# Eight split-weight buffers at eight starting offsets, and convolution taps halved in place

## The chip, the cores and the metric

The kernel runs on one core of a Trainium2 chip. The metric is the device time of one execution in microseconds. An execution of the program is also taken with the hardware profiler; its span reaches from the first to the last instruction, and the device time of that execution is a little longer.

## The reference

Four trunk layers work on 256 latent tokens and 256 context tokens of 1024 channels. Layers 0 and 3 mix tokens with a two-directional state-space scan, layer 1 with windowed attention, layer 2 with a chunked gate; each is followed by a gated feed-forward part. Everything is float32. Cut to what matters here:

```python
for i in range(DEPTH):                       # 4
    a = modulate(rms_norm(h, norm_g[i, 0]), sh1, sc1)
    h = h + g1 * mixer[i % 3](a)             # scan, attention, gate
    h = h + g2 * swiglu(modulate(rms_norm(h, norm_g[i, 1]), sh2, sc2), ffn_w_in[i], ffn_w_out[i])
return rms_norm(h_lat, final_g)

# inside the scan mixer, before the scan:
xbc = silu(depthwise_conv(zxbcdt[..., 2048:5120], conv_w, conv_b))   # 5 taps along the tokens
```

## The kernel before

**Products in three.** A float32 product is made of three products of a shorter format (F32R). A weight `w` is split into `hi`, which is `w` rounded to that format, and `lo = w - hi`; an activation is split in the same way. `mm3` (lines 163 to 167) issues, for each 128 x 128 block of weights, `hi` with the activation's high part (L165), `hi` with its low part (L166) and `lo` with its high part (L167). In the value parts of layers 1 and 2 (tile `vp`) the split weights are the moving operand and the activations the stationary one; everywhere else the weights are the stationary one, and 512 or 256 (258 in one stage) token columns stream past.

**The order of the weights.** `make_plan` lists all 454 weight chunks of the program in the order of use. `get(idx)` (L158) hands out one chunk's buffers and first calls `pump` (L143), which brings the chunks up to two ahead: a DMA into one of 3 `raw` buffers (L140), then, in pieces of 512 columns, a cast on ScalarE into `hi` (L152) and a subtraction into `lo` (L154) on VectorE, in the scan stages partly on GpSimd. There are 4 `hi` and 4 `lo` buffers of 1024 words, taken in turn, so a buffer is rewritten four chunks later, once the products that read it are done.

**Where the buffers lie.** All offsets are bytes within a partition. The three `raw` buffers start at 45056, 49152 and 53248, the four `hi` at 57344, 61440, 65536 and 69632, the four `lo` at 73728, 77824, 81920 and 86016, the split activations `a_hi` and `a_lo` at 90112 and 106496. All these are multiples of 2048, and so are the tiles of the stages behind them (`hh`, `hl`, `gh`, `gl`, `xw`, `bm` and others, from 122880 on). Tiles are laid end to end, rounded up to 32 bytes. The scan stage's small tiles end at 229312 of 229376.

**The taps.** The parameters lie in the tile `par`, brought by the first DMA (L115). Its columns from `C_CW` to `C_NW` hold the taps and biases of the convolution: 5 x 24 taps for each of the two scan layers, then 24 biases for each, 288 columns in all. `ssd_scan` makes a tile `hw` of 6 x 24 columns with six multiplications by 0.5 (L746 to L749), once in layer 0 and once in layer 3. `conv` (L751) reads its taps and bias from `hw`, one column as a scalar for each instruction: a ScalarE activation (L757), four VectorE instructions (L761), and then `y (1 + tanh y)`, for which the half is wanted.

**Order of instructions.** The kernel is written as a data flow; a scheduler puts each engine's instructions in order by priority and estimated time and may pull an instruction with no unmet need far ahead of its place in the text. Each engine then works through its queue in order.

Of the kernel before, what the change touches and what calls it, by code (L numbers as in the profile page):

```python
# [8 lines left out]
F32 = mybir.dt.float32  # L9
F32R = mybir.dt.float32r  # L10
# [3 lines left out]
ALU = mybir.AluOpType  # L14
# [3 lines left out]
P = 128  # L18
# [47 lines left out]
SC_MM = (3,)  # L66
SC_FROM = 4
SPLIT_BUFS = 4
TAIL_POOL = (5, 7)


# [3 lines left out]
C_CW = C_FG + 8  # L75
C_CB = C_CW + 2 * 5 * 24
C_NW = C_CB + 2 * 24
# [22 lines left out]
class Builder:  # L100
    def __init__(self, ctx, tc, ap):
        self.ctx, self.tc, self.nc, self.ap = ctx, tc, tc.nc, ap
        nc = self.nc
        pool = lambda name, bufs=1, **kw: ctx.enter_context(tc.tile_pool(name=name, bufs=bufs, **kw))
        self.cp = pool("cp")
        self.sp = pool("sp", 2)
        self.wp = pool("wp")
        self.dp = pool("dp", space=bass.MemoryType.DRAM)
        self.pm = pool("pm", 3, space=PSUM)
        self.ps = pool("ps", 3, space=PSUM)  # L110
        self.pt = pool("pt", 2, space=PSUM)
        cp = self.cp

        self.par = cp.tile([P, NPAR + PAD], F32, name="par")[:, :NPAR]
        nc.sync.dma_start(self.par, ap["pars"])  # L115
        self.k0 = cp.tile([P, NK0], F32, name="k0")
        nc.sync.dma_start(self.k0, ap["consts"][:, 0:NK0])
        self.h = [cp.tile([P, KD, HT], F32, name=f"h{i}") for i in range(2)]
        for i in range(2):
            nc.sync.dma_start(self.h[i], ap["xin"][i])  # L120
        self.ident = self.k0[:, K_ID : K_ID + P]
        self.ones = self.k0[:, K_ONE : K_ONE + P]
        self.a_hi = self.a_lo = None
        self.acc, self.sqlast = {}, None

        self.plan = []
        self.ready = {}
        self.emitted = 0
        self.ahead = 2
        self.lo_eng = nc.vector  # L130
        self.lo_alt = None
# [11 lines left out]
    def pump(self, upto):  # L143
        nc = self.nc
        while self.emitted < min(upto + 1, len(self.plan)):
            src, n = self.plan[self.emitted]
            raw = self.load(src, n)
            hi = self.wp.tile([P, 1024], F32R, tag="hi", name="hi", bufs=SPLIT_BUFS)
            lo = self.wp.tile([P, 1024], F32R, tag="lo", name="lo", bufs=SPLIT_BUFS)
            for p0 in range(0, n, PIECE):  # L150
                sl = slice(p0, min(n, p0 + PIECE))
                nc.scalar.copy(hi[:, sl], raw[:, sl])  # L152
                eng = self.lo_eng if self.lo_alt is None or p0 == 0 else self.lo_alt
                eng.tensor_tensor(out=lo[:, sl], in0=raw[:, sl], in1=hi[:, sl].bitcast(F32), op=ALU.subtract)  # L154
            self.ready[self.emitted] = (hi, lo)
            self.emitted += 1
# [540 lines left out]
    def ssd_scan(self, layer, jj, lat_only, sp, first, turn_out):  # L697
        nc = self.nc
        par = self.par
# [42 lines left out]

        turn = []


        hw = self.ss.tile([P, 6, 24], F32, name="hw")  # L746
        for k in range(6):
            c = C_CW + (jj * 5 + k) * 24 if k < 5 else C_CB + jj * 24
            nc.vector.tensor_scalar(hw[:, k, :], par[:, c : c + 24], 0.5, None, ALU.mult)  # L749

        def conv(t, a, b, o, dst):  # L751
            w = lambda k: hw[:, k, t : t + 1]
            y = dst
            nh = (b - a) // HT
            yv = y[:, a:b].rearrange("p (h t) -> p h t", h=nh)
            ov = o.rearrange("p (h t) -> p h t", h=nh)
            nc.scalar.activation(y[:, a:b], o, AF.Identity, bias=w(5), scale=w(2))  # L757
            for k in (0, 1, 3, 4):
                s = k - 2
                d0, d1 = max(0, -s), HT - max(0, s)  # L760
                nc.vector.scalar_tensor_tensor(  # L761
                    yv[:, :, d0:d1], ov[:, :, d0 + s : d1 + s], w(k), yv[:, :, d0:d1], ALU.mult, ALU.add
                )
            th = sp.tile([P, T], F32, tag="xt", name="th", bufs=SS_BUFS["xt"])[:, a:b]
            nc.scalar.activation(th, y[:, a:b], AF.Tanh)
            nc.vector.scalar_tensor_tensor(y[:, a:b], th, 1.0, y[:, a:b], ALU.add, ALU.mult)

        def epi_x(m, a, b, o):
            xt = sp.tile([P, T], F32, tag="xt", name="xt", bufs=SS_BUFS["xt"])
            conv(m, a, b, o, xt)  # L770
            flush()
            turn.append((m, a, b, xt))
# [14 lines left out]
        def bc(i):  # L787

            def epi(m, a, b, o):
                flush()  # L790
                tag = ("bt", "ct")[i % 2]
                dst = (bt, ct)[i % 2][i // 2] = sp.tile([P, T], F32, tag=tag, name=tag, bufs=SS_BUFS[tag])
                conv(16 + 4 * (i % 2) + i // 2, a, b, o, dst)
                mod_step()

            self.linear([ids["bc"][i]], range(KD), self.rhs_a, epi, toks=tlat if i % 2 else ((0, T),))
# [57 lines left out]
        for d in range(2):  # L854
            w = self.ss.tile([P, 4, 32], F32, name=f"wdt{d}")
# [549 lines left out]
    def build(self):  # L1405
# [69 lines left out]
        for m in range(KD):  # L1475
            fg = self.par[:, C_FG + m : C_FG + m + 1]
            if m in TAIL_POOL:
                nc.gpsimd.tensor_scalar(o[:, m, :], self.h[LAT][:, m, :], fg, None, ALU.mult)
# [126 lines left out]
```

## Time and profile before

| | |
|---|---|
| median of 3 runs | 2669.74 us (2665.63 to 2680.74) |
| the profiled execution | 2673.48 us |
| its span | 2671.7 us |
| TensorE products / weight loads, count | 13672 / 13672 |
| mean granted TensorE clock | 0.990 |
| DMA moved | 353.57 MB, 132 GB/s in the mean |

In the profile, PE is TensorE's products and PEld its weight loads, DVE is VectorE, ACT ScalarE, POOL GpSimd, SP the queue that issues the DMAs. A line number such as L165 is a line of the kernel before. In a group's row, `out<-in` names the tiles, `x` the count, and the two numbers behind the bar are the busy time in us and the mean of one in ns. A row of the timeline has the start, the time in us, the engine, the line and the operation, and in brackets the idle time of the engine before it and what ended it. The time of one product in a row overlaps with that of the next, since products are pipelined; how fast they follow each other is read from their starts. A row of one tile's instructions has the shortest, the median and the longest time in ns. A row of busy time by windows has, for each engine, busy us and the number of instructions.

### The profile page before, as it was taken

To read this page: it belongs to the slowest core of one execution; us is meant where nothing else is said; L and a number is where in the kernel's file an instruction comes from. 1 tells how busy PE (TensorE), PEld (TensorE's weight loads), DVE (VectorE), ACT (ScalarE), POOL (GpSimd) and SP (SyncE) were. 2 spreads that over 40 slices of the span, in tenths; PEclk is the share of its full clock that TensorE was granted. 3 is DMA by queue.
4 is the path that set the end of the run, shared out by engine and by line. 5 is a ranking of instruction groups with operands and counts; after the bars stand their busy time and mean duration, and the time that the engine had idled before them with its cause. 6 is when DMAs were issued, how large, how long until landed. Compare 5 with 4: busy or idle time off the path is not lost. (4 is left out here: it accounts for less than half of the span.)

```text
span 2671.7 us, 37274 instructions
## 1 busy us (share of the span) xinstructions
PE 2579.9 (97%) x13672; PEld 2089.5 (78%) x13672; DVE 1951.7 (73%) x3825; ACT 1104.9 (41%) x2281; POOL 379.0 (14%) x334
## 2 busy tenths in 40 slices
PE   6999999899999999999999999999999989999998
PEld 3666668888788854888888888898888877669998
DVE  4799998885865775584956664578577579998776
ACT  4556553332223555332223432342222355555444
POOL 3322423200001034100000000010000133341001
PEclk9999999999999999999999999999999999999999
DMA  6521125464644420264644232236455322215554
GB/s 236 169 84 55 56 71 174 134 228 135 213 159 133 127 72 9 80 213 128 216 160 143 100 104 87 87 127 204 145 188 189 97 90 77 73 64 174 182 182 127
DMA packets 105894, 353.57 MB, mean 132 GB/s; under 512 B 14064, under 2 KB 15728, under 8 KB 105456
## 3 DMA queue, kind: packets, MB, share of 16 engines
q1 hardware_dynamic: 105712, 351.20, 40.1%
q8 instruction: 108, 1.77, 0.3%
q14 instruction: 74, 0.61, 0.1%
HBM read 344.46 MB, written 1.44 MB: 129 GB/s over the span
## 5 line engine op out<-in xcount | busy, mean ns | idle before, releaser
L165 PE MATMUL mm<-a_hi,hi 128*128 128x512 f32 (+2 forms) x2512 | 898.3, 359 | 8.1 <-ACT a_hi L299 6.0
L166 PE MATMUL mm<-a_lo,hi 128*128 128x512 f32 (+2 forms) x2512 | 895.4, 357 | 2.6 <-DVE a_lo L300 2.6
L167 PE MATMUL mm<-a_hi,lo 128*128 128x512 f32 (+2 forms) x2512 | 895.6, 357 | 0.0
L152 ACT CAST hi<-raw 128x512 fp32r<-128x512 f32 (+1 forms) x906 | 522.5, 610 | 892.4 <-PE mm L166 517.3
L154 DVE TENSOR_TENSOR lo<-raw,hi 128x512 fp32r<-128x512 f32 (+1 forms) x794 | 547.6, 709 | 108.8 <-ACT hi L152 103.4
L165 PEld LDWEIGHTS mm<-a_hi,hi 128*128 128x128 f32 x2512 | 473.0, 189 | 90.3 <-issue 16.4
L167 PEld LDWEIGHTS mm<-a_hi,lo 128*128 128x128 f32 x2512 | 474.1, 189 | 74.5 <-issue 10.5
L166 PEld LDWEIGHTS mm<-a_lo,hi 128*128 128x128 f32 x2512 | 474.1, 189 | 74.2 <-issue 7.3
L414 DVE SCALAR_TENSOR_TENSOR mj<-mw,cb 128x1024 bf16<-128x1024 f32 x320 | 398.2, 1244 | 54.3 <-DMA mw<-in_w_modT 46.7
L253 POOL TENSOR_TENSOR sqacc<-sqacc,sqt 128x256 f32<-128x256 f32 x77 | 72.1, 944 | 1658.2 <-ACT sqt L248 1656.1
L258 DVE SCALAR_TENSOR_TENSOR h<-mm,mod,h 128x256 f32<-128x256 f32 x216 | 97.4, 480 | 268.8 <-PE mm L167 268.8
L165 PE MATMUL mm<-hh,hi 128*128 128x512 f32 (+1 forms) x788 | 271.0, 344 | 2.1 <-ACT hh L207 2.0
L166 PE MATMUL mm<-hl,hi 128*128 128x512 f32 (+1 forms) x788 | 271.5, 345 | 1.6 <-DVE hl L208 1.6
L167 PE MATMUL mm<-hh,lo 128*128 128x512 f32 (+1 forms) x788 | 270.6, 344 | 0.0
L154 POOL TENSOR_TENSOR lo<-raw,hi 128x512 fp32r<-128x512 f32 x112 | 161.8, 1454 | 246.9 <-ACT hi L152 245.1
L165 PEld LDWEIGHTS mm<-hh,hi 128*128 128x128 f32 x788 | 149.5, 190 | 21.3 <-ACT hh L207 3.8
L166 PEld LDWEIGHTS mm<-hl,hi 128*128 128x128 f32 x788 | 149.7, 190 | 20.3 <-DVE hl L208 2.8
L167 PEld LDWEIGHTS mm<-hh,lo 128*128 128x128 f32 x788 | 149.7, 190 | 17.5
L167 PE MATMUL mm<-gh,lo 128*128 128x256 f32 (+1 forms) x376 | 125.8, 335 | 9.1 <-DVE lo L154 9.1
L165 PE MATMUL mm<-gh,hi 128*128 128x256 f32 (+1 forms) x376 | 125.7, 334 | 0.0
L166 PE MATMUL mm<-gl,hi 128*128 128x256 f32 (+1 forms) x376 | 125.6, 334 | 0.0
L207 ACT CAST hh<-sg 128x512 fp32r<-128x512 f32 (+1 forms) x94 | 51.0, 543 | 143.0 <-DVE sg L459 129.1
(248 smaller groups left out, 3069.7 us busy)
## 6 DMA issues: line engine op xcount, KB each, us to landing
raw<-in_w_f SPq DMA_DIRECT2D x208, 512.0 KB
mw<-in_w_modT SPq DMA_DIRECT2D x160, 512.0 KB
raw<-in_w_f SPq DMA_DIRECT2D x64, 448.0 KB
raw<-in_w_xbc SPq DMA_DIRECT2D x48, 512.0 KB
raw<-in_w_z SPq DMA_DIRECT2D x32, 512.0 KB
raw<-in_w_so SPq DMA_DIRECT2D x32, 512.0 KB
mw<-in_w_mod SPq DMA_DIRECT2D x16, 512.0 KB
raw<-in_w_mod SPq DMA_DIRECT2D x16, 512.0 KB
```

Source lines behind the costliest of these rows:

```text
L152: nc.scalar.copy(hi[:, sl], raw[:, sl])
L154: eng.tensor_tensor(out=lo[:, sl], in0=raw[:, sl], in1=hi[:, sl].bitcast(F32), op=ALU.subtract)
L165: nc.tensor.matmul(out, wh, xh, start=first, stop=False)
L166: nc.tensor.matmul(out, wh, xl, start=False, stop=False)
L167: self.last_mm = nc.tensor.matmul(out, wl, xh, start=False, stop=last).ins
L207: nc.scalar.copy(hi, src)
L253: eng.tensor_tensor(out=self.acc[hf], in0=self.acc[hf], in1=t, op=ALU.add)
L258: self.nc.vector.scalar_tensor_tensor(h, src, g[:, hf, m : m + 1], h, ALU.mult, ALU.add)
L414: nc.vector.scalar_tensor_tensor(junk, w, 1.0, self.cb[:, v, :], ALU.mult, ALU.mult, accum_out=self.mod[layer][:, seg, v, j : j + 1])
```

## The change

The eight buffers get a tag of their own each, with 1032 words instead of 1024, and the slice that is used begins 0 or 4 words into it, by the table `SPLIT_SHIFT`. Chunk `i` uses the buffers `i mod 4`, as in turn before. The taps and biases of both layers are multiplied by 0.5 where they lie, in one instruction behind the load of `par`; the tile `hw` goes, and `conv` reads columns of `par`.

```diff
+SPLIT_SHIFT = ((0, 0), (4, 4), (0, 0), (0, 4))
@@ __init__
         nc.sync.dma_start(self.k0, ap["consts"][:, 0:NK0])
+
+        cw = self.par[:, C_CW:C_NW]
+        nc.vector.tensor_scalar(cw, cw, 0.5, None, ALU.mult)
@@ pump
             raw = self.load(src, n)
-            hi = self.wp.tile([P, 1024], F32R, tag="hi", name="hi", bufs=SPLIT_BUFS)
-            lo = self.wp.tile([P, 1024], F32R, tag="lo", name="lo", bufs=SPLIT_BUFS)
+
+            i = self.emitted % SPLIT_BUFS
+            t = [self.wp.tile([P, 1032], F32R, tag=f"{nm}{i}", name=f"{nm}{i}", bufs=1) for nm in ("hi", "lo")]
+            hi, lo = (t[q][:, s : s + 1024] for q, s in enumerate(SPLIT_SHIFT[i]))
@@ ssd_scan
-        hw = self.ss.tile([P, 6, 24], F32, name="hw")
-        for k in range(6):
-            c = C_CW + (jj * 5 + k) * 24 if k < 5 else C_CB + jj * 24
-            nc.vector.tensor_scalar(hw[:, k, :], par[:, c : c + 24], 0.5, None, ALU.mult)
-
         def conv(t, a, b, o, dst):
-            w = lambda k: hw[:, k, t : t + 1]
+
+            def w(k):
+                c = (C_CW + (jj * 5 + k) * 24 if k < 5 else C_CB + jj * 24) + t
+                return par[:, c : c + 1]
+
             y = dst
```

## The prediction

> **What bounds the kernel now.** I read the page's first part, then the busy time by windows, then the timeline of one dense stretch, then the groups by line with shapes kept apart.
>
> ```profile
> span 2671.7 us, 37274 instructions
> PE 2579.9 (97%) x13672; PEld 2089.5 (78%) x13672; DVE 1951.7 (73%) x3825; ACT 1104.9 (41%) x2281; POOL 379.0 (14%) x334
> ```
>
> ```profile
> 1200.00:1300.00 100.00, 100.00 (x442) 82.78 (x442) 63.92 (x115) 27.03 (x48) 0.00 (x0) 1.00 0.49 160
> 2500.00:2600.00 100.00, 99.89 (x827) 99.49 (x826) 69.52 (x148) 48.16 (x92) 0.00 (x0) 1.00 0.59 180
> 100.00:500.00 400.00, 377.50 (x1839) 270.13 (x1838) 368.46 (x616) 203.24 (x425) 124.97 (x88) 0.99 0.32 104
> 2100.00:2400.00 300.00, 277.08 (x1598) 213.77 (x1597) 254.92 (x465) 162.66 (x353) 105.51 (x84) 0.99 0.23 76
> ```
>
> The columns after the window are PE, PEld, DVE, ACT, POOL, then the granted clock. TensorE is the bound: it is full in the feed-forward stages (first two rows), and only in the two scan stages (last two) does it leave about 23 us each, where DVE is busy 92% and 85%. So the splitting of weights, which is work of ACT, DVE and POOL, can set the end only in the scan stages, or by slowing TensorE itself. The timeline shows whether it does the latter.
>
> ```profile
> 640.00 0.39 PE L167 MATMUL mm<-hh,lo 128*128 128x512 f32 x1
> ...
> 640.88 1.14 ACT L152 CAST hi<-raw 128x512 fp32r<-128x512 f32 x2 [4.30 <-PE mm L166]
> ...
> 641.90 1.28 DVE L154 TENSOR_TENSOR lo<-raw,hi 128x512 fp32r<-128x512 f32 x2
> ...
> 642.72 0.39 PE L167 MATMUL mm<-hh,lo 128*128 128x512 f32 x1
> ...
> 645.44 0.39 PE L167 MATMUL mm<-hh,lo 128*128 128x512 f32 x1
> ```
>
> Products go in threes, so twelve products start between the first and second PE row, and twelve between the second and third. Both stretches take 2.72 us, 226.7 ns a product. In the first, ACT writes a `hi` buffer and DVE reads it and writes a `lo`; in the second neither does. At the offsets of before, where every one of these buffers starts at a multiple of 4096 bytes, the writers cost TensorE nothing that the trace resolves.
>
> ```profile
> 2519.90 0.28 PE L167 MATMUL mm<-hh,lo 128*128 128x256 f32 x1
> ...
> 2521.70 0.28 PE L167 MATMUL mm<-hh,lo 128*128 128x256 f32 x1
> ```
>
> With 256 columns, fifteen products take 1.80 us, 120.0 ns each. From 256 to 512 columns is 106.7 ns, or 0.4167 ns a column, and both widths leave the same rest: 226.7 - 213.3 = 13.3 ns and 120.0 - 106.7 = 13.3 ns. This rest is the only place in the dense stages where an address could matter, and the rivals turn on it.
>
> **The change part by part.** *New places.* A buffer of 1032 words has 4128 bytes, 16 x 256 + 32. Laid end to end from byte 57344 (a multiple of 256) in the order `hi0, lo0, hi1, lo1, ...`, and with the shifts of 4 words (16 bytes), the slices start at 0, 32, 80, 112, 128, 160, 192 and 240 within 256 bytes. What follows moves by 8 x 32 = 256 bytes, so the right-hand operands keep their place within 256. Buffers were already used in turn, four of each kind, so which product must finish before a buffer is rewritten stays the same: no wait is added.
>
> *Price of one split.* The writers are these:
>
> ```profile
> L152 ACT CAST hi<-raw x906: 498/618/651, 26.6 to 2650.7; 128x512 fp32r<-128x512 f32 x169, 128x384 fp32r<-128x384 f32 x13
> L154 DVE TENSOR_TENSOR lo<-raw,hi x794: 545/684/1812, 126.8 to 2651.4; 128x512 fp32r<-128x512 f32 x199
> ```
>
> ```profile
> L154 DVE TENSOR_TENSOR lo<-raw,hi 128x512 fp32r<-128x512 f32 (+1 forms) x794 | 547.6, 709 | 108.8 <-ACT hi L152 103.4
> ```
>
> ACT's 906 casts lie within 498 to 651 ns over two widths; there is no tail that a collision could explain. DVE has a tail to 1812 ns, and its mean of 709 lies 25 ns over the median of 684: 794 x 25 = 20 us of DVE in all, which is the most that could be won here if the tail came from the offsets. Whether an odd start costs DVE anything is seen at the convolution, whose taps read and write at starts shifted by 0, 1 or 2 words:
>
> ```profile
> L761 DVE SCALAR_TENSOR_TENSOR xt<-mm,hw,xt 128x510 f32<-128x510 f32 x56 | 41.5, 741 | 0.7
> L761 DVE SCALAR_TENSOR_TENSOR xt<-mm,hw,xt 128x508 f32<-128x508 f32 x56 | 41.4, 738 | 9.6 <-ACT xt L757 9.3
> L1336 DVE SCALAR_TENSOR_TENSOR s<-sv,par,bt 128x512 f32<-128x512 f32 x16 | 11.9, 744 | 0.0
> ```
>
> 744 ns for 512 elements from an unshifted start, 741 for 510 and 738 for 508: the time follows the count, and the shifts cost nothing. I take 0 for each split, by these rows, which are the ones that show a shifted start. The bounds: 20 us won with the tail, 3 ns lost on each of 794 subtractions, 2.4 us, and of either only the part in the scan stages could be seen.
>
> *Taps.* Twelve multiplications of 24 columns go.
>
> ```profile
> 0.84 0.27 DVE L1414 MEMSET cm<- 128x256 f32 x1 [0.84 <-PEq L1593]
> 1.06 0.06 DVE L1468 MEMSET eps<- 128x1 f32 x1
> ...
> 2.01 0.20 ACT L1470 ACTIVATE root<-eps 128x1 f32<-128x1 f32 x1
> 2.23 1.28 ACT L1412 ACT_TABLE_LOAD   x1
> ...
> 3.56 0.58 DVE L749 TENSOR_SCALAR hw<-par 128x24 f32<-128x24 f32 x6 [2.44 <-DMA par<-in_pars]
> 4.05 0.24 DVE L1416 COPY cm<-cs 128x8 f32<-128x8 f32 x2
> ...
> 13.25 1.08 PE L352 MATMUL macc<-mw,cm 128*32 128x256 f32 x8 [13.25 <-DMA mw<-in_w_mod]
> ```
>
> The first six take 0.58 us from the landing of the parameters. In their place comes one multiplication of 288 columns: at least 0.10 us, which is 0.58 shared among six, and at most the 0.74 us of 510 columns. In proportion to the columns that is 0.10 + 0.64 x 264/486 = 0.45 us, which I take: the copies to `cm` start about when they did. Nobody needs `cm` before 13.25 us, where the first product waits for its weights' DMA: a cover of 9 us. Should the multiplication stand ahead of the two memsets in DVE's queue, then `eps`, ACT's root and its table load slip behind the landing: 3.56 + 0.74 + 0.33 (memsets) + 0.20 + 1.28 is 6.1 us, and `cs` and `cm` (0.24) behind it end before 7, still within the cover. Zero.
>
> ```profile
> 1074.47 0.41 DVE L749 TENSOR_SCALAR hw<-par 128x24 f32<-128x24 f32 x4
> 1076.02 0.29 DVE L208 TENSOR_TENSOR a_lo<-pv,a_hi 128x128 fp32r<-128x128 f32 x1 [1.13 <-ACT a_hi L207]
> 1076.23 0.25 DVE L749 TENSOR_SCALAR hw<-par 128x24 f32<-128x24 f32 x2
> 1076.64 0.29 DVE L208 TENSOR_TENSOR a_lo<-pv,a_hi 128x128 fp32r<-128x128 f32 x1 [0.17 <-ACT a_hi L207]
> ```
>
> The last layer's six were pulled forward into the attention stage, where DVE waits for ACT after them, 1.13 and 0.17 us. Taking them out lengthens those waits. Zero. The convolution reads its scalar from `par` in place of `hw`, with the same instructions at the same widths. Zero.
>
> **Sum.** 0 for the buffers, 0 for the taps: the profiled execution, 2673.48 us (span 2671.7 and 1.8 around it), stays as it is. It lies 3.7 us above the median of 2669.74, and the median is what I forecast from: 2669 us. Since the instructions of DVE's queue are laid out anew, their order in the scan stages may differ slightly; the three runs of before spread from 2665.63 to 2680.74 us, and I allow the forecast 2660 to 2680.
>
> **Rival 1, faster: the 13.3 ns are a collision of two reads.** A weight slice and the right-hand slice both start at a multiple of 256 bytes in every split product. If TensorE's two reads meet in the same part of the memory because of that, most offsets part them. For it speaks a row of unsplit products:
>
> ```profile
> 2274.55 1.72 PE u L905 x4
> ```
>
> Four products of 512 columns take 430 ns each. At two passes of 0.4167 ns a column that is 426.7 + 3.3, so 10 ns of the 13.3 are peculiar to the split kind. Against it: the operands of `u` also start at multiples of 2048 bytes and have no such rest; and 512 columns have no more of it than 256, while collisions should grow with the stream. The price goes by these counts:
>
> ```profile
> L165 PE MATMUL mm<-a_hi,hi 128*128 128x512 f32 (+2 forms) x2512 | 898.3, 359 | 8.1 <-ACT a_hi L299 6.0
> L165 PE MATMUL mm<-hh,hi 128*128 128x512 f32 (+1 forms) x788 | 271.0, 344 | 2.1 <-ACT hh L207 2.0
> L165 PE MATMUL mm<-gh,hi 128*128 128x256 f32 (+1 forms) x376 | 125.7, 334 | 0.0
> ```
>
> Three lines of 3676 are 11,028 products. At most 3437 (1839 + 1598) lie in the scan stages, which DVE bounds in part. With seven of eight buffers off the common start, 10 ns x 7/8 on 7591 to 11,028 products is 66 to 96 us: 2573 to 2603 us. If only the buffers far from the common start gain, it may be a fifth of that, 2655 us.
>
> The Trainium skill, TensorE: Matmul & The Clock Gate, section Back-to-back issue gap, gives the distance of bf16 products as N / 2.4 + 2.5 ns; by it 512 columns would take about 216 ns where this trace has 226.7, and the sum would lose about 11 ns a product. Against the rival stands its page SBUF — State Buffer, section Who interferes with whom: TensorE's two read ports are independent, and "PE and ACT never wait on anyone". By that page nothing is to be won here, and the equal stretches of 2.72 us agree with it as far as writers go; no row shows weights at another offset. Chance 0.15.
>
> **Rival 2, slower: a slice that starts off the old boundary takes longer to load.** It would show in the stages of 256 columns, where the weight loads fill 99.49 of 100 us (the window from 2500), while with 512 columns 17 us of 100 are free.
>
> ```profile
> 2270.37 0.44 PE xtp L781 x4
> ```
>
> A 128-column load with its product can follow the last in 110 ns, 10 ns less than the 120 of the narrow products, so a load decides from 10 ns more on, or at once if those 10 ns are already taken up by it. If a slice of 512 bytes comes in pieces as large as the shift, 32 of 16 bytes, one more would be 110 / 32 = 3.4 ns (an estimate); a stall as large as today's rest 13.3.
>
> ```profile
> L166 PE MATMUL mm<-a_lo,hi 128*128 128x256 f32 x512 | 145.6, 287 | 0.8 <-DVE a_lo L300 0.8
> L165 PE MATMUL mm<-a_hi,hi 128*128 128x258 f32 x352 | 99.9, 284 | 0.0
> L165 PE MATMUL mm<-hh,hi 128*128 128x256 f32 x344 | 97.2, 283 | 0.1
> L165 PE MATMUL mm<-gh,hi 128*128 128x256 f32 x208 | 60.0, 288 | 0.0
> ```
>
> 1416 x 3 = 4248 narrow products, 7/8 of them off the boundary, are 3717: 13 us at 3.4 ns (2682 us), 49 us at 13.3 (2718). Against it: all starts are still multiples of 16 bytes. Chance 0.11.
>
> **Rival 3: the starts don't differ.** Were each buffer rounded up to 256 bytes, only the 16-byte shifts would remain. The memory speaks against it: 64 bytes are free at the top, the taps' tile gives back 576, and eight buffers rounded up would need 2048. Its time is the forecast's.
>
> **How the numbers follow.** No change has 0.74 with rival 3 in it, rival 1 0.15, rival 2 0.11. Within 0.5% (2656 to 2683 us; about what a measurement of this kernel can tell from no change) I count 0.71 of the first and 0.01 of the third case; 0.02 of the first goes to faster, 0.01 to slower. That makes 0.17 faster, 0.72 the same, 0.11 slower. The range reaches from 2640, the small form of rival 1, to 2690, the small form of rival 2.
>
> **What would show it.** Right: the products of 512 and 256 columns still follow each other at 226.7 and 120.0 ns, the casts stay at 618 and DVE's subtractions at 684 ns in the median, one multiplication of 288 columns stands near 3.6 us and none in the attention stage. Rival 1 shows as a shorter distance with more than 442 products in a full window of 100 us; rival 2 as fewer than 827 in a window of the last stage. I am wrong if the distance between products depends on which buffer feeds them.

## The result: 0.7% slower, and the profile after

Eighteen runs of the changed kernel have a median of 2689.58 us (2684.94 to 2702.80); eighteen of the kernel before 2672.07 us (2665.63 to 2686.36). The ratio is 1.0066, with a 95% interval of 1.0051 to 1.0081: about 17.6 us slower. The forecast was 2669 us and no change. The profiled execution took 2684.94 us, with a span of 2683.2 us at a mean granted clock of 0.992, against 2673.48, 2671.7 and 0.990 before. So the clock isn't the reason.

The first part of the page of the kernel after:

```profile
span 2683.2 us, 37271 instructions
PE 2601.9 (97%) x13672; PEld 2081.8 (78%) x13672; DVE 1945.0 (72%) x3814; ACT 1105.4 (41%) x2281; POOL 377.1 (14%) x334
```

PE does the same 13672 products and is busy 22 us longer. DVE has eleven instructions fewer (twelve multiplications of taps went, one came). The windows show in which stages PE lost time (a product that reaches into a window counts in it, so 100 us hold one or two more than fit by their starts):

```profile
100.00:500.00 400.00, 382.97 (x1861) 272.97 (x1860) 365.03 (x625) 204.25 (x427) 120.34 (x87) 0.99 0.32 103
1200.00:1300.00 100.00, 100.00 (x432) 80.77 (x431) 57.74 (x104) 25.98 (x46) 0.00 (x0) 1.00 0.47 150
...
2500.00:2600.00 100.00, 99.83 (x832) 99.42 (x831) 71.02 (x155) 49.18 (x95) 0.00 (x0) 1.00 0.57 179
```

In the full window of 512 columns there are 432 products where there were 442; in the window of 256 columns 832 where there were 827. The wide products follow each other more slowly, the narrow ones faster. In the scan stage from 100 us more products are done than before (1861 against 1839). The timeline of the kernel after gives the distances themselves:

```profile
640.42 0.39 PE L173 MATMUL mm<-hh,lo 128*128 128x512 f32 x1
...
643.22 0.39 PE L173 MATMUL mm<-hh,lo 128*128 128x512 f32 x1
...
2530.21 0.28 PE L173 MATMUL mm<-hh,lo 128*128 128x256 f32 x1
...
2531.98 0.28 PE L173 MATMUL mm<-hh,lo 128*128 128x256 f32 x1
```

Between the first two rows lie twelve products: 2.80 us, 233.3 ns each, where it was 226.7. Between the last two lie fifteen: 1.77 us, 118.0 ns, where it was 120.0. L171, L172 and L173 after are L165, L166 and L167 before. The writers, and the one multiplication that is left of the taps:

```profile
L158 ACT CAST hi<-raw x906: 501/618/652, 24.3 to 2661.8; 128x512 fp32r<-128x512 f32 x169, 128x384 fp32r<-128x384 f32 x13
L160 DVE TENSOR_TENSOR lo<-raw,hi x794: 545/685/1804, 123.6 to 2662.5; 128x512 fp32r<-128x512 f32 x199
```

```profile
3.61 0.31 DVE L121 TENSOR_SCALAR par<-par 128x288 f32<-128x288 f32 x1 [2.49 <-DMA par<-in_pars]
3.85 0.25 DVE L1420 COPY cm<-cs 128x8 f32<-128x8 f32 x2
```

Median 618 ns again for the casts, 685 where it was 684 for the subtractions; the tail of DVE (1804 ns) is still there, so it didn't come from the offsets. The copies to `cm` start 0.20 us earlier than before.

**Where the time came from.** PE does the same products in the same order in both traces, so the time from the start of each product to the start of the next can be subtracted one by one. All terms together are 11.8 us, and the span grew by 11.5. The medians lie 17.5 us apart; the profiled execution of the kernel after is the fastest of its eighteen, so about 6 us of the difference are not in this account:

| products | count | after minus before, us | each, ns |
|---|---|---|---|
| 512 columns, following closely | 6780 | +36.05 | +5.32 |
| 512 columns, further apart | 456 | -12.81 | |
| 256 columns, following closely | 3281 | -5.51 | -1.68 |
| 258 columns, following closely | 1052 | -0.44 | -0.42 |
| all others | 2102 | -5.5 | |

With 512 columns, closely means that the starts are at most 233 ns apart before; with 256 and 258, that they are at most about 130 ns apart in both traces. Of the 456 wide products further apart, 188 lie at 234 to 240 ns; the other 268 stand before a wait and hold 12.1 of the 12.8 us.

The whole loss is in the wide products that follow closely. A third of it is given back where PE has to wait for another engine anyway: a product that ends later makes the wait behind it shorter.

### The profile page after: what moved, and what is told of

Read it like the earlier page. It is cut to its first block, busy times and chain, and to the rows that moved or that the text cites. A ratio compares the mean times of both kernels' runs of the same rounds, so it can differ in the third digit from the quotient of the medians.

```text
span 2683.2 us, 37271 instructions
## 1 busy us (share of the span) xinstructions
PE 2601.9 (97%) x13672; PEld 2081.8 (78%) x13672; DVE 1945.0 (72%) x3814; ACT 1105.4 (41%) x2281; POOL 377.1 (14%) x334
## 3 DMA queue, kind: packets, MB, share of 16 engines
q8 instruction: 108, 1.77, 0.3%
## 5 line engine op out<-in xcount | busy, mean ns | idle before, releaser
L171 PE MATMUL mm<-a_hi,hi 128*128 128x512 f32 (+2 forms) x2512 | 902.8, 361 | 8.5 <-ACT a_hi L305 6.1
L172 PE MATMUL mm<-a_lo,hi 128*128 128x512 f32 (+2 forms) x2512 | 904.4, 361 | 2.9 <-DVE a_lo L306 2.9
L173 PE MATMUL mm<-a_hi,lo 128*128 128x512 f32 (+2 forms) x2512 | 900.1, 359 | 0.0
L171 PEld LDWEIGHTS mm<-a_hi,hi 128*128 128x128 f32 x2512 | 470.9, 188 | 100.4 <-issue 16.6
L172 PEld LDWEIGHTS mm<-a_lo,hi 128*128 128x128 f32 x2512 | 472.5, 188 | 81.0 <-issue 7.3
L173 PEld LDWEIGHTS mm<-a_hi,lo 128*128 128x128 f32 x2512 | 472.5, 188 | 80.7 <-issue 10.6
L172 PE MATMUL mm<-hl,hi 128*128 128x512 f32 (+1 forms) x788 | 272.8, 346 | 0.4 <-DVE hl L214 0.3
L171 PE MATMUL mm<-hh,hi 128*128 128x512 f32 (+1 forms) x788 | 271.2, 345 | 0.1
L173 PE MATMUL mm<-hh,lo 128*128 128x512 f32 (+1 forms) x788 | 271.0, 344 | 0.0
L171 PEld LDWEIGHTS mm<-hh,hi 128*128 128x128 f32 x788 | 147.9, 188 | 21.1 <-ACT hh L213 0.5
L172 PEld LDWEIGHTS mm<-hl,hi 128*128 128x128 f32 x788 | 148.1, 188 | 20.7 <-DVE hl L214 1.3
L173 PEld LDWEIGHTS mm<-hh,lo 128*128 128x128 f32 x788 | 148.2, 188 | 19.5
L173 PE MATMUL mm<-gh,lo 128*128 128x256 f32 (+1 forms) x376 | 126.2, 336 | 7.3 <-DVE lo L160 7.3
L172 PE MATMUL mm<-gl,hi 128*128 128x256 f32 (+1 forms) x376 | 126.2, 336 | 0.0
L171 PE MATMUL mm<-gh,hi 128*128 128x256 f32 (+1 forms) x376 | 125.9, 335 | 0.0
L765 DVE SCALAR_TENSOR_TENSOR xt<-mm,par,xt 128x508 f32<-128x508 f32 (+3 forms) x144 | 98.2, 682 | 12.7 <-ACT xt L761 11.0
```

The lines of the kernel that those rows point to most:

```text
L171: nc.tensor.matmul(out, wh, xh, start=first, stop=False)
L172: nc.tensor.matmul(out, wh, xl, start=False, stop=False)
L173: self.last_mm = nc.tensor.matmul(out, wl, xh, start=False, stop=last).ins
L765: nc.vector.scalar_tensor_tensor(yv[:, :, d0:d1], ov[:, :, d0 + s : d1 + s], w(k), yv[:, :, d0:d1], ALU.mult, ALU.add)
```

## The experiments

**Theory:** the distance between products depends on where the weight slice starts relative to the right-hand slice, within 256 bytes, and on nothing else of the change. **Rivals:** the writers, now at other offsets, disturb TensorE's reads; the taps, or another order of instructions that they bring, cost the time; the slices' own offset counts, not their place relative to the other operand.

**`taps`: the taps alone.** The kernel before, with the change's lines on the taps and `hw` and without those on the buffers.

> The taps alone: before, with the taps halved in place and the eight buffers as they were. Theories 1 and 2 (the offsets cost the time): 2672 us, ratio 1.000 within 0.002, products at 226.7 and 120.0 ns. Theory 3 (the taps or the order of instructions cost it): 2690 us, ratio 1.006.

2672.69 us, ratio 1.0005 (0.9989 to 1.0021). The taps cost nothing; the loss belongs to the buffers.

**`map`: products alone.** A kernel of nothing but groups of 96 products, in threes as in `mm3`; the weights of a group start at one offset, the right-hand slices at multiples of 2048 bytes. No other engine works.

```diff
+wh = mem[:, d + k * P : d + (k + 1) * P]            # d: the group's offset
+wl = mem[:, 1536 + d + k * P : 1536 + d + (k + 1) * P]
```

> The kernel's own computation is left out: it runs only split products on fixed data, in groups of 96 (32 blocks of three products), each group with another starting offset of the weight slices from 0 to 1024 bytes, the right-hand slices fixed, first 29 groups with 512 columns, then 29 with 256; nothing else runs beside TensorE. Theory 1 (the two reads of TensorE meet: the distance between products depends on where the weight slice lies relative to the right-hand slice): at offset 0 226.7 and 120.0 ns, at other offsets up to 234 and down to 114 ns, and 512 and 1024 the same as 0. Theory 2 (the writers of the buffers, ACT and DVE, meet TensorE's reads at the new places): with no writer all groups at 226.7 and 120.0 ns, within 1 ns.

The first products of the groups at 0, 16, 32 and 48 bytes with 512 columns, then the group at 64 bytes with 256 columns and the one behind it:

```profile
37.20 0.39 PE L132 MATMUL waa<-mem 128*128 128x512 f32 x1
...
58.73 0.39 PE L131 MATMUL wab<-mem 128*128 128x512 f32 x1
...
80.50 0.39 PE L131 MATMUL wac<-mem 128*128 128x512 f32 x1
...
102.89 0.40 PE L131 MATMUL wad<-mem 128*128 128x512 f32 x1
...
725.91 0.28 PE L131 MATMUL nae<-mem 128*128 128x256 f32 x1
...
736.80 0.28 PE L131 MATMUL naf<-mem 128*128 128x256 f32 x1
```

From the second row to the third are 96 products in 21.77 us, 226.8 ns each (16 bytes); from the third to the fourth 22.39 us, 233.2 ns (32 bytes). The last two rows, 10.89 us, give 113.4 ns (64 bytes, 256 columns). The mean of each group, in ns:

| offset, bytes | 0 | 16 | 32 | 48 | 64 | 80 | 96 | 128 | 160 | 192 | 208 | 240 | 256 |
|---|---|---|---|---|---|---|---|---|---|---|---|---|---|
| 512 columns | 226.7 | 226.8 | 233.2 | 233.3 | 233.3 | 231.9 | 234.2 | 233.4 | 233.3 | 229.0 | 231.8 | 226.9 | 226.7 |
| 256 columns | 119.9 | 118.4 | 118.3 | 117.8 | 113.4 | 118.8 | 118.7 | 118.6 | 119.9 | 117.8 | 116.7 | 119.9 | 119.9 |

From 256 on the values repeat within 0.3 ns, 512 and 1024 bytes being as 0; the exceptions are 480 and 496 bytes with 256 columns, 117.8 and 117.3 ns where 224 and 240 have 116.7 and 119.9. The effect of the change, with both signs, is there with no writer at work: that rival falls.

**`right256`: everything behind the buffers moved by 256 bytes.** `taps`, with 64 unused words behind the eight old buffers.

```diff
+gap = self.wp.tile([P, 64], F32, name="gap")
```

> The taps in place and the eight buffers as before, all at multiples of 4096 bytes, but 256 unused bytes behind them, so that all right-hand operands start 256 bytes later. Theory 1 with a period over 256 bytes: products of 512 columns go from 226.7 to about 230 ns although no weight buffer has moved, 2680 to 2695 us. Theory 1 with a period of 256 bytes, theory 2 and theory 3 without taps' cost: 2672 us and 226.7 ns.

2671.92 us, ratio 0.9997 (0.9984 to 1.0009). The 256 bytes by which the change moves what follows cost nothing. Counted as in the table above, the wide products that follow closely give +1.5 us in the profile of `taps` and +1.9 us in this one, so such a term is good to about 2 us.

**`eight_same512`: the change with these 256 bytes once more.**

> The changed kernel with 256 more unused bytes behind the eight buffers, so that the right-hand operands start at a multiple of 512 again as before, with the weight buffers at the same eight places as in the change. Theory 1 with a period over 256 bytes: the distances differ from the change's 231 to 234 ns for 512 columns, by 2 ns or more in the mean, and the time by 10 us or more. Theory 1 with a period of 256, and theory 2: as the change, 2690 us, 231 to 234 ns.

2689.60 us, ratio 1.0070 (1.0048 to 1.0092), as the change. The loss doesn't hang on how far the operands lie apart beyond 256 bytes.

**`all32`: both operands moved together.** The constant `PAD`, the words of a tile ahead of all of them, goes from 80 to 88.

> Before, with 32 more unused bytes in front of the raw buffers, so that raw, hi, lo and all right-hand operands start 32 bytes off a multiple of 256 and keep their distances. Theory 1 (the distance between weights and right-hand operand decides): 2672 us, ratio 1.000 within 0.002, products at 226.7 and 120.0 ns. Theory of the boundary (a slice that starts off a multiple of 256 costs more): 512 columns at about 233 ns and 2690 us or more.

2675.52 us, ratio 1.0014 (1.0001 to 1.0028), and the products still follow at 226.7 and 119.9 ns; its window has 443 wide products, the kernel before 442:

```profile
1200.00:1300.00 100.00, 100.00 (x443) 82.84 (x442) 62.17 (x112) 26.54 (x47) 0.00 (x0) 1.00 0.50 158
```

So a slice's own offset is not what counts.

**`right32`: the old buffers, the other operand moved.** The kernel before with 8 unused words behind the buffers: all eight stay where they were, and what they are multiplied with moves by 32 bytes.

> Before, with 32 unused bytes behind the eight buffers, which stay at multiples of 4096: only the right-hand operands move, by 32 bytes. Theory 1: as the first map at 224, 512 columns at 233.3 and 256 at 116.7 ns, so at most 7236 x 6.6 - 4488 x 3.3 = 33 us more: 2685 to 2705 us. Theory that the weights' own start decides: 2672 us and 226.7 ns.

2701.06 us, ratio 1.0105 (1.0092 to 1.0118). Its windows:

```profile
1200.00:1300.00 100.00, 100.00 (x431) 80.31 (x430) 59.38 (x107) 25.99 (x46) 0.00 (x0) 1.00 0.46 150
2500.00:2600.00 100.00, 99.76 (x836) 99.39 (x835) 72.53 (x170) 52.12 (x99) 0.00 (x0) 1.00 0.57 179
```

431 and 836 products: slower than the change with wide products, faster with narrow ones. The buffers weren't touched, and the kernel loses more than by the change. With `all32` this shows that the relative place decides.

**`map2`: `hi` and `lo` at different offsets**, 16 x 16 pairs, groups of 48 products, otherwise as `map`.

> The kernel's own computation is left out: split products on fixed data alone, in 256 groups of 48 for each width (512, then 256 columns); the hi slices start at one of 16 offsets (0 to 240 bytes in steps of 16) and the lo slices at one of 16, the right-hand slices stay. Theory 1 (each load of weights meets the right-hand read that runs beside it, by their distance within 256 bytes): groups with equal offsets repeat the first map (226.7 at 0, 16 and 240, about 233.3 at most others; 113.4 at 64 for 256 columns), and mixed groups lie near the mean of the two, two thirds hi and one third lo, within 3 ns. A theory in which hi and lo matter by their distance from each other: mixed groups at up to 240 ns where each alone has 227.

The expectation that a mixed group lies near the mean of its two offsets failed. Below are the first products of the pairs (0, 32) and (0, 48), then those of (0, 144) and (0, 160), all with 512 columns:

```profile
47.36 0.39 PE L131 MATMUL wac<-mem 128*128 128x512 f32 x1
...
58.55 0.40 PE L131 MATMUL wad<-mem 128*128 128x512 f32 x1
...
125.31 0.39 PE L131 MATMUL waj<-mem 128*128 128x512 f32 x1
...
136.19 0.39 PE L131 MATMUL wak<-mem 128*128 128x512 f32 x1
```

The pair (0, 32), two loads of three at the best offset, takes 11.19 us for 48 products, 233.1 ns each and not 229. But the pair (0, 144) takes 10.88 us, 226.7 ns, though 144 alone, the pair (144, 144), has 233.3; so a load at another offset doesn't always cost something, and a mixed group can't be told from the two offsets alone. The change's four pairs, (0, 32), (80, 112), (128, 160) and (192, 240), have 233.2, 233.3, 233.3 and 229.0, in the mean 232.2, and 118.3 with 256 columns. The kernel after has 232.2 and 118.2 in the mean over products that follow closely.

**`lo32`: only `lo` moved by 32 bytes**, `hi` and the operands at a distance of 0 (`taps` with 8 unused words between the `hi` and `lo` buffers and 56 behind them).

> The taps in place; the four hi buffers keep the distance 0, the four lo buffers move by 32 bytes (the right-hand operands by 256). One load in three is off. If each load pays for itself: 2.2 ns a product of 512 columns, 229 ns and 2682 us. By the second map (hi 0, lo 32: 233.3 and 118.4 ns), where one load in three spoils all: 6.6 ns on 6780 products, 44.7 us, less 5, of which seven eighths: 2705 us.

2701.03 us, ratio 1.0106 (1.0084 to 1.0128): as dear as `right32`, which moved all of them. One load in three at 32 bytes spoils the three; pricing each load by itself is wrong here.

**`right64`: the operands moved by 64 bytes**, so that the weights lie 192 bytes from them (`taps` with 16 unused words).

> The taps in place and 64 unused bytes behind the eight buffers, which stay at multiples of 4096: the right-hand operands move by 64, so the weights start 192 bytes beyond them within 256. By the maps (229.0 and 117.8 ns at 192): 2.3 ns on 6780 dense products of 512 columns, 15.6 us, less 2.2 ns on 3266 of 256, 7.2 us, and of the 8.4 us the seven eighths that came through with the operands moved by 32 bytes: about 7 us, 2679 us, ratio 1.003. A theory in which every offset but 0 costs the same: 2701 us.

2678.36 us, ratio 1.0023 (1.0008 to 1.0039): as the map has it, a smaller loss with 512 columns (+16.2 us, counted as in the table of the change) and the gain with 256 (-9.1 us).

**`narrow64`: one offset for each width.** The kernel before; in the last layer, where the products have 256 and 258 columns, the right-hand slices are moved within their tiles by 192 bytes, so that the weights lie 64 bytes from them. All products of 512 columns stay at 0.

```diff
+RAW_OFF = 48
+LAT_BACK = 16
-        self.split(self.a_hi[:, m, :HT], self.a_lo[:, m, :HT], ...)
+        sl = slice(RAW_OFF, RAW_OFF + HT)
+        self.split(self.a_hi[:, m, sl], self.a_lo[:, m, sl], ...)
-                    self.split(hid[i][0][:, a:b], hid[i][1][:, a:b], s)
+                    d = LAT_BACK if last else 0
+                    self.split(hid[i][0][:, a - d : b - d], hid[i][1][:, a - d : b - d], s)
```

> Before, with the right-hand slices of the last layer's feed-forward part and output projection (256 and 258 columns) moved by 192 bytes within their tiles, so that the weights start 64 bytes beyond them within 256; nothing else moves. Theory 1: these 1968 products go from 120 to 113.4 ns, 13 us, if the DVE and the DMAs keep up: 2659 us, ratio 0.995. Theory that this holds only with nothing running beside TensorE: 2672 us.

2669.68 us, ratio 0.9983 (0.9971 to 0.9996): faster, by a third of what was expected. The products of 258 columns stayed at 120.8 ns, and those of 256 showed two distances, near 113.3 and near 117.8 ns.

**`all16` and `best`: all eight slices at 16 bytes**, in `best` with the last layer as in `narrow64`. The eight buffers are slices of one tile, so that all can have the same odd start. What these kernels leave out is the order that eight tiles enforce: a slice may be rewritten before products that want its old weights, so their output is not that of the kernel before.

```diff
+self.all = self.wp.tile([P, 8 * 1024 + 64], F32R, name="all")
+q = 4 + 1024 * (self.emitted % SPLIT_BUFS)
+hi, lo = (self.all[:, q + d : q + d + 1024] for d in (0, 1024 * SPLIT_BUFS))
```

> The taps in place; the eight buffers are slices of one tile and start 16 bytes off a multiple of 256, the right-hand operands on one. By the first map at 16: 512 columns at 226.7 ns as before, 256 at 118.4 in place of 119.9, which is 1.5 ns on 3266 products: 5 us less at most, 2667 to 2672 us. If the order of DVE's queue, which is laid out anew, costs more than that: over 2675 us.

> The same with the last layer's right-hand slices of 256 and 258 columns moved so that the weights lie 64 bytes beyond them. By the maps: the 5 us of the 16 bytes, and 2 to 6.5 ns on the 912 products of 256 columns of the last layer, 2 to 6 us: 2661 to 2668 us, ratio 0.996 to 0.999. If the gains don't add: as the kernel with 16 bytes alone.

Both missed: 2698.57 us, ratio 1.0098 (1.0068 to 1.0127), and 2699.38 us, 1.0081 (1.0051 to 1.0111). The windows of `all16` show why the map didn't carry over:

```profile
430.00:450.00 20.00, 20.00 (x90) 16.55 (x89) 18.35 (x24) 5.06 (x11) 10.37 (x7) 1.00 0.60 190
640.00:660.00 20.00, 20.00 (x88) 16.18 (x87) 7.20 (x13) 4.41 (x8) 0.00 (x0) 1.00 0.34 106
1660.00:1680.00 20.00, 20.00 (x90) 16.56 (x89) 7.96 (x15) 4.34 (x7) 0.00 (x0) 1.00 0.32 106
1900.00:1920.00 20.00, 20.00 (x88) 16.18 (x87) 7.19 (x13) 4.34 (x7) 0.00 (x0) 1.00 0.34 106
```

At one and the same distance of 16 bytes and with 512 columns throughout, 20 us hold 90 products in some stretches and 88 in others; from the starts it is 226.7 and 233.3 ns, and each lasts for long stretches. From 1150 to 1480 us the 512-column products that follow closely, averaged over 50 us at a time, never leave 233.3 to 233.4 ns; from 430 to 480 us they are at 226.7.

**`map3`: does it matter what came before?** Groups as in `map`, in an order that brings 16 bytes once behind 0 and once behind 32; then groups that begin behind a wait.

> Left out: everything but groups of 96 split products (the kernel's output is not computed). First thirteen groups of 512 columns follow each other without a break, at the distances 0, 16, 32, 16, 0, 16, 240, 32, 240, 0, 240, 32, 0; eight of 256 columns at 0, 64, 0, 128, 64, 32, 64, 0; then groups at 0, 16, 32, 64, 240 (512 columns) and 0, 64 (256 columns), each behind a wait for ACT and one product of another width, eight widths in all. Theory 1 (one offset has two lasting states, and what comes before the stretch decides): 16 behind 0 keeps 226.7 ns, 16 and 240 behind 32 stay at about 233.3, 0 is 226.7 behind anything; behind the waits 0 is always 226.7, 32 always 233.3, and 16, 240, and 64 with 256 columns show both values. Theory 2 (the offset alone decides, and the writers of the full kernel disturb it): 16 and 240 are 226.7 to 227 in every group, and 64 with 256 columns 113.4 in every group.

The first products of the groups at 0, 16, 32, 16, 0, 16, 240, 32, 240 and 0 bytes:

```profile
36.65 0.39 PE L141 MATMUL paao0e<-mem 128*128 128x512 f32 x1
...
58.19 0.39 PE L140 MATMUL pabo16e<-mem 128*128 128x512 f32 x1
...
79.95 0.39 PE L140 MATMUL paco32e<-mem 128*128 128x512 f32 x1
...
102.35 0.40 PE L140 MATMUL pado16e<-mem 128*128 128x512 f32 x1
...
124.75 0.39 PE L140 MATMUL paeo0e<-mem 128*128 128x512 f32 x1
...
146.51 0.39 PE L140 MATMUL pafo16e<-mem 128*128 128x512 f32 x1
...
168.27 0.39 PE L140 MATMUL pago240e<-mem 128*128 128x512 f32 x1
...
190.04 0.39 PE L140 MATMUL paho32e<-mem 128*128 128x512 f32 x1
...
212.43 0.39 PE L140 MATMUL paio240e<-mem 128*128 128x512 f32 x1
...
234.35 0.39 PE L140 MATMUL pajo0e<-mem 128*128 128x512 f32 x1
```

From each row to the next are 96 products (from the first row 95). The group at 16 bytes takes 21.76 us behind 0 and 22.40 us behind 32: 226.7 and 233.3 ns at the same offset, and its own 96 products don't bring it back. The group at 0 behind it takes 21.76 us again: at 0 the distance returns to 226.7 whatever came before. The group at 240 bytes takes 21.77 us behind 16 and 21.92 us, 228.3 ns, behind 32. Behind a wait, over eight groups each: 0 always ends at 226.7 and 32 at 233.3 ns; 16 was at 226.7 twice and at 233.3 six times; 240 at 226.7 five times and at 228.3 three times; 64 bytes with 256 columns at 113.3 four times and at 117.8 four times. This is theory 1 of the expectation, for each of its points but one: 240 bytes behind 32 goes to 228.3, not 233.3.

**`all0`: the one tile without the odd start.** `all16` with `q` beginning at 0, so that all distances are 0.

> The kernel all16 with its eight slices at distance 0 in place of 16 bytes; as there, a slice of the one tile may be rewritten before products that want the old weights, so these take other weights; count, shapes and order of all instructions are those of all16. If the distance of 16 bytes costs the time there, this one is at the time of before, 2667 to 2677 us, with products at 226.7 and 119.9 ns. If the single tile or its waits cost it, 2690 to 2705 us.

2685.34 us, ratio 1.0042 (1.0025 to 1.0059), between the two expectations. Its products have the old distances, as the window shows; below it is `all16`'s:

```profile
1200.00:1300.00 100.00, 100.00 (x443) 82.83 (x442) 63.98 (x114) 29.83 (x50) 0.00 (x0) 1.00 0.48 155
```

```profile
1200.00:1300.00 100.00, 100.00 (x431) 80.96 (x430) 60.05 (x106) 27.39 (x46) 0.00 (x0) 1.00 0.46 149
```

So `all16` lost in two ways: some 13 us by the one tile (2685.34 against 2672.64, the kernel before beside it), and another 13 by the distance (2698.57 against 2685.34, from two sets of runs). Product by product in order of their starts, `all0` falls behind the kernel before in steps: by 6.6 us up to 338 us, again between 1486 and 1597 us (from 4.0 to 10.7) and between 2112 and 2192 us (from 9.5 to 16.0), and not within the dense stages between them. At the second PE waits, and at all three the granted clock is lower. For the second, the row of `all0`, then that of the kernel before:

```profile
1490.00:1500.00 10.00, 7.06 (x37) 5.78 (x37) 9.80 (x30) 4.59 (x11) 0.00 (x0) 0.86 0.24 66
```

```profile
1490.00:1500.00 10.00, 10.00 (x46) 7.72 (x45) 8.40 (x28) 4.65 (x8) 0.00 (x0) 1.00 0.34 111
```

From 1500 to 1520 us the clock is 0.90 against 1.00, from 260 to 300 us 0.96 and from 2140 to 2160 us 0.83, both against 1.00. Over the whole span it is 0.983 to 0.987 in the four runs of `all0`, and 0.988 to 0.992 in the seven of the kernel before. Half a per cent of 2672 us is 13 us (an estimate that takes TensorE as the bound throughout), as much as the one tile costs; it doesn't tell what a wait cost and what the clock behind it. Some 850 of the 13672 products also stand at another place in the order than before. Which of this comes first isn't settled. `all16` has the same order as `all0` and a clock of 0.987 to 0.989, so the order and the clock don't explain the 13 us between these two.

**`narrow192`: the last layer at 192 bytes.** `narrow64` with `RAW_OFF = 16` and `LAT_BACK = 48`.

> The kernel narrow64 with the last layer's right-hand slices moved by 64 bytes in place of 192, so that the weights lie 192 bytes from them; products of 512 columns stay at distance 0. In right64, where all products have this distance, the 1392 products of 256 columns behind 2180 us took 4.6 us less than in before and the 1056 of 258 columns 1.9 us less. If these carry over, the kernel gains 6.5 us, ratio 0.9975 (2665 us by a before of 2672), with more than 840 products in the window from 2500 to 2600 us. If waits for weights give it back, or the state that a stretch enters is another than in right64, the ratio is 0.999 to 1.001.

2667.82 us, ratio 0.9973 (0.9954 to 0.9992), the fastest of all. Its windows:

```profile
1200.00:1300.00 100.00, 100.00 (x443) 82.81 (x442) 61.33 (x110) 27.21 (x49) 0.00 (x0) 1.00 0.50 161
2500.00:2600.00 100.00, 99.81 (x841) 99.41 (x840) 70.56 (x148) 48.48 (x92) 0.00 (x0) 1.00 0.60 184
```

443 wide products, where the kernel before has 442, and 841 narrow ones for 827. In its profile the products of 256 and 258 columns that follow closely gave 3.9 us and the span is 5.2 us shorter, a little less than the 6.5 expected. With intervals this wide it is not shown to be faster than `narrow64`; each is shown to be faster than the kernel before, and both lie below the kernel after.

## Why the prediction was wrong, point by point

- **The bound** was right: PE is busy for 97% of both spans, and what happens between its products sets the time. That a slower product is absorbed in the scan stages was seen too: from 100 to 500 and from 2120 to 2400 us the wide products that follow closely cost 5.7 us, and all products together took 1.3 us less. Waits in other stretches gave time back as well.
- **New places** were right: the slices start at the offsets that were worked out, and the right-hand operands moved by 256 bytes, which costs nothing (`right256`).
- **The price of one split**, 0, was right: medians of 618 and 685 ns. The 20 us in DVE's tail were not of the offsets.
- **Taps**, zero, was right: `taps` alone is 1.0005. The multiplication took 0.31 us, within the bounds of 0.10 and 0.74 and below the 0.45 taken.
- **The failed step is "0 for the buffers".** The term priced the writing of the buffers and left out their being read: it took for granted that the distance between products doesn't depend on where the weights lie. It does, by +5.32 ns on 6780 wide products and -1.68 ns on 3281 narrow ones. The prediction named this as the point by which it would be wrong, and said that no row shows weights at another offset; from there to a price of zero there was no row, only the arguments against the rivals. The runs show in its place 226.7 ns at a distance of 0 and 232.2 in the mean of the change's four pairs.
- **Rival 1** had the right quantity, the relative start within 256 bytes of the two slices that TensorE reads, and the wrong sign for 512 columns. It took the 13.3 ns rest for the price of the common start. In fact no offset in the maps is faster than the common start for 512 columns; the rest is 20 ns at most other offsets. For 256 columns it was right in a small way: the rest falls from 13.3 to about 11.3 ns. The argument against it, that 512 columns have no more rest than 256, holds only at 0; elsewhere the two widths in the main go opposite ways.
- **Rival 2** had the right sign and the wrong stage and mechanism. It put the loss where loads fill the time, with 256 columns; there the kernel became faster, and the loss is where loads have 17 us of 100 free.
- **Rival 3**, that the starts don't differ, is out: they do.
- **The size** against the forecast is 2689.6 - 2669 = 20.6 us. 3.1 us of it is the reference: the median of before was 2672.07 in eighteen runs. Of the other 17.5 us, the account of the two profiled executions shows 11.8, and by it the loss is the term above.

The Trainium skill, SBUF — State Buffer, section Who interferes with whom, gives TensorE two independent read ports and says that PE doesn't wait on anyone. As far as other engines go, the runs agree: in the full kernel and with no other engine at work the distances are the same. For the two reads of TensorE itself the measurement differs: 226.7 or 233.3 ns by the relative place of weights and right-hand slice.

**What stays open.** That the two reads meet in some part of the memory that repeats every 256 bytes fits the period, but no run shows the memory. Why 0 holds one distance, 16, 64 and 240 bytes two, and why one load in three at 32 bytes spoils the others and at 144 does not, is not settled; nor why 258 columns hardly answer to 64 bytes (120.8 ns) where 256 columns may fall to 113.3.

## What to carry to other kernels

Before the start of a buffer is changed, look at both operands of the products that read it, not only at who writes it: what counts is their distance within 256 bytes, and it can be changed by a few unused words behind a tile. Where all tiles begin at multiples of 256 bytes, as here, products of 512 columns already follow each other as fast as anywhere in the maps; a stage of narrower products can be tried by itself, and gained 0.3% here. A small kernel of the instruction alone tells the prices, but it has to bring each case behind different predecessors and behind waits, or it shows one of two lasting values as if it were the only one.

## What the runs showed of the hardware that was not expected

- The distance between split products depends on the weights' start relative to the right-hand slice with a period of 256 bytes: 226.7 ns at 0 and 233.2 to 233.4 at most other offsets with 512 columns; 119.9 at 0, 116.7 to 118.8 at most others and 113.4 at 64 with 256 columns. In the main, wide and narrow products go opposite ways.
- There are lasting rhythms: at a distance of 16 bytes the same products follow at 226.7 or at 233.3 ns, in groups without a break by what came before the group; there it ended only with another offset or a wait. Over three products these are 680 and 700 ns.
- A group of three with one load at 32 bytes and two at 0 goes at 233.1 ns, as if all three were at 32; with the one load at 144 bytes it goes at 226.7, as if all three were at 0.
